# Halo V summed chunk by chunk, half of the FFN weights cast DRAM to DRAM ahead of use, and V scratch on the sync queue, in a hybrid decoder layer on eight cores

## The chip, the cores and the metric

The kernel runs as one program on the eight NeuronCores of one Trainium2 chip (two dies of four cores). The metric is the device time of the slowest core, in microseconds. A run is called slow when one die runs over 1% longer at a lower granted TensorE clock, or when the run is over 1.5% above the fastest of its kernel; ratios and intervals use fast runs alone.

## The reference, cut to what matters

One decoder layer on x of shape (4, 8192, 1024). Each core takes half a sequence: 8 "own" tiles of 512 tokens, preceded by 4 "halo" tiles, of which only K and V are needed.

```python
h = rmsnorm(x, g_mix)
q, k, v, u, qm = split(h @ w_in, ...)            # 512, 512, 512, 256, 256 columns
y_attn = dilated_window_attention(q, k, v)       # (128,1), (512,4), (2048,16), merged
y_pool = causal_multiscale_pool(u) @ w_pool * pool_scale
y_mem  = softmax(qm @ km.T) @ vm                 # km, vm from 256 memory tokens
x = x + concat(y_attn, y_pool, y_mem) @ w_out
x = x + relu(rmsnorm(x, g_ffn) @ w_ff1)**2 @ w_ff2   # 1024 -> 4096 -> 1024
return rmsnorm(x, g_final)
```

## The kernel before

Weights come in pieces of 128 x 4096 values. A piece is 2 MiB in f32 in DRAM (`wall`) and 1 MiB in bf16. A ring of three slots in SBUF holds the pieces. The first use of a piece is a casting load from `wall` on the POOL queue; it is then written back as bf16 to a DRAM scratch (`sc`), and later uses are bf16 loads on the sync (SP) queue. Half of the FFN pieces are not written back at their first use ("deferred"), so they are loaded from f32 twice, in the first and the second own tile.

```python
deferred = {P_FF1 + i for i in range(1, 8, 2)} | {P_FF2 + i for i in range(1, 8, 2)}
def ring_issue():
    ...
    if idx in done:
        T.dma("sp", ring_sem[s], ring[s][:], sc[idx], reads=[b_scp[idx]], writes=[b_ring[s]])
    else:
        T.dma("pool", cast_sem[s], ring[s][:], wall[idx], writes=[b_ring[s]])
        if idx in deferred:
            deferred.discard(idx)
            return
        done.add(idx)
        T.dma("sp", wb_sem[s], sc[idx], ring[s][:], reads=[b_ring[s]], writes=[b_scp[idx]])
```

V is needed in two token orders. From the last halo tile on, each of four V blocks is evicted from PSUM, written to a DRAM scratch `vs` (192 KB each) and read back in the other order into `Vd4` (768 KB). Attention of a tile cannot use its own Vd4 before this read has landed.

```python
T.dma("pool", vsw_sem[b], vs[j % 2][b * 128:(b + 1) * 128, :], dst, reads=bd, ...)   # four times
...
def read_v():
    for t_ in toks:                      # the four writes
        T.wait("pool", t_)
    T.dma("pool", vsr_sem[j % 2], Vd4[:, slot, :, :].rearrange("p r e -> p (r e)"),
          vs[j % 2].rearrange("(c r) e -> c (r e)", r=4), ...)
```

`T.wait` and `T.dma` run in program order on the queue's own engine: a wait holds up everything that this engine issues later (in the change, below, the sync queue on core 1 issued nothing from 125.2 to 173.95 us while it waited for writes of V). Every tile starts with a LayerNorm-like statistic (`LN`: squares on ACT, adds on DVE, one matmul with ones, then norms on DVE). A halo tile then runs four V groups of eight matmuls and four K groups.

The softmax here doesn't subtract the row's maximum and nothing guards it: scores larger than these inputs give would overflow.

## Time and profile before

1661.23 us, median of 3 runs (1658.43 to 1662.81). TensorE is busy for 93% of the span, and from 480 us on for about 98% of each 200 us, so the loss sits in the first 480 us.

The rows of the page for TensorE and the DMA engines, in 40 equal slices of 41.5 us; a digit is the busy share in tenths:

```profile
PE   3889899989799999999999999999999999998996
...
PEclk9999999999999999999999999999999999998998
DMA  9828578995857675354835375344734373434342
```

The first slice is a third busy, and slices 9 and 11 (332 to 374 and 415 to 457 us) dip. The reasons are in the waits of TensorE on the slowest core, core 1 (what it waited for: us in total, times, longest):

```profile
PE mm L336 <- DVE acc L362: 38.9, 8, 19.5
...
PE mm L336 <- DMA ring<-wall: 9.9, 3, 4.7
PE mm L336 <- DMA ring<-wscratch: 9.4, 2, 7.3
```

It waits 38.9 us for the LayerNorm sum (19.5 of it at the start), and 19.3 us for weights in the ring. The timeline of TensorE shows where (start, duration, instruction, count; in brackets the idle time before it and what ended it):

```profile
341.44 1.89 PE L336 MATMUL mm<-aT,ring 128*128 128x512 bf16 x8 [1.94 <-DMA ring<-wall]
...
370.11 9.90 PE L336 MATMUL mm<-aT,ring 128*128 128x512 bf16 x32 [4.65 <-DMA ring<-wall]
...
435.82 3.61 PE L336 MATMUL mm<-h2T,ring 128*128 128x512 bf16 x16 [3.34 <-DMA ring<-wall]
...
451.65 4.95 PE L336 MATMUL mm<-h2T,ring 128*128 128x512 bf16 x16 [7.35 <-DMA ring<-wscratch]
```

These four gaps are 17.3 us. The matmuls after the 4.65 us gap took 9.90 us for 32, where 32 take 7.07 us elsewhere. The granted clock, from the trace by stretch, was 0.71 over these 9.90 us: 0.50 from 370.1 to 375.6, where in the kept trace the matmuls start 0.427 us apart, and 0.97 from there to 380.0, where they start 0.216 us apart. So about 5.5 us went at half rate. After the 7.35 us gap the clock was 0.50 for 2.5 us, and 16 matmuls took 4.95 us; after the 3.34 us gap it was 1.00, and 16 took 3.61 us.

### The profile page before, as it was taken

The numbers are of one execution on the slowest core, as the hardware profiler recorded it, in microseconds if no ns is written. First come the engines' busy times: TensorE is split into PE (matmuls) and PEld (weight loads), VectorE is DVE, ScalarE is ACT, GpSimd is POOL, SyncE is SP. The second block draws the span as 40 slices with busy tenths as digits, with TensorE's granted clock in tenths as the row PEclk, the third lists the DMA queues.
The fourth block names the chain that finished last, engine by engine and source line by source line (L and its number), as shares of the span: only waits on it lengthen the run. The fifth ranks groups of instructions, "written<-read, shape, count | busy, mean of one in ns | idle before, by whom it ended". The sixth has DMA issues, their size and how long they took to land.

```text
span 1660.2 us, 27812 instructions; the slowest of 8 cores (1640.5 to 1660.2 us)
## 1 busy us (share of the span) xinstructions
PE 1548.5 (93%) x9722; PEld 748.0 (45%) x9722; DVE 930.2 (56%) x1383; ACT 715.5 (43%) x1069; POOL 137.2 (8%) x189
## 2 busy tenths in 40 slices
PE   3889899989799999999999999999999999998996
PEld 1434544444355444454454444454445444453442
DVE  5666566546365466656465556656565555546333
ACT  3545654532444336443444436343444335442221
POOL 1102110101000010000100010000100000000000
PEclk9999999999999999999999999999999999998998
DMA  9828578995857675354835375344734373434342
GB/s 227 227 87 263 131 153 165 198 203 174 245 152 201 180 219 200 105 176 138 276 107 178 110 233 178 128 153 166 253 114 167 128 234 122 163 130 152 139 152 90
DMA packets 41081, 282.93 MB, mean 170 GB/s; under 512 B 5248, under 2 KB 5376, under 8 KB 8560
## 3 DMA queue, kind: packets, MB, share of 16 engines
q1 hardware_dynamic: 24048, 172.01, 30.6%
q0 software_dynamic: 16896, 109.13, 25.6%
q8 instruction: 81, 1.33, 0.3%
q14 instruction: 56, 0.46, 0.1%
HBM read 266.77 MB, written 46.92 MB: 189 GB/s over the span
## 4 chain that ended last, share of the span: by engine, by line
PE 80%; DMA 7%; DVE 5%; issue 4%; ACT 4%; ACTq 0%; DVEq 0%; POOL 0%; SPq 0%; POOLq 0%
PE mm L336 70%; PE ob L577 6%; PE sc L554 4%; DMA ring<-wall 3%; DMA ring<-wscratch 2%; ACT P L556 2%; DVE acc L362 1%; ACT sq L360 1%; DMA wscratch<-ring 1%; DVE val L588 1%; DMA out<-X 1%; DVE X L709 1%; DVE X L374 0%; DMA cpc_t<-cpc 0%; ACT rt L686 0%
## 5 line engine op out<-in xcount | busy, mean ns | idle before, releaser
L336 PE MATMUL mm<-h2T,ring 128*128 128x512 bf16 x2192 | 511.0, 383 | 13.9 <-DMA ring<-wscratch 7.3
L336 PE MATMUL mm<-aT,ring 128*128 128x512 bf16 x2048 | 474.2, 382 | 24.5 <-DVE X L709 15.9
L689 DVE TENSOR_TENSOR aT<-rt 128x512 bf16<-128x512 f32 x256 | 199.9, 783 | 242.6 <-ACT rt L686 241.1
L556 ACT ACTIVATE P<-sc 128x1024 bf16<-128x1024 f32 x256 | 247.7, 1023 | 184.4 <-PE sc L554 178.7
L336 PEld LDWEIGHTS mm<-h2T,ring 128*128 128x128 bf16 x2192 | 206.7, 98 | 256.3 <-issue 32.7
L336 PEld LDWEIGHTS mm<-aT,ring 128*128 128x128 bf16 x2048 | 192.6, 98 | 249.5 <-issue 42.8
L686 ACT ACTIVATE rt<-mm 128x512 f32<-128x512 f32 x256 | 153.0, 598 | 272.2 <-PE mm L336 250.7
L561 DVE TENSOR_TENSOR P<-P,E 128x1024 bf16<-128x1024 bf16 x224 | 154.0, 694 | 127.6 <-ACT P L556 126.5
L360 ACT ACTIVATE sq<-X 128x512 f32<-128x512 f32 x196 | 122.4, 630 | 161.3 <-DVE X L709 102.5
L362 DVE TENSOR_TENSOR acc<-acc,sq 128x512 f32<-128x512 f32 (+1 forms) x203 | 142.9, 705 | 73.6 <-ACT sq L360 71.1
L336 PE MATMUL mm<-hT,ring 128*128 128x512 bf16 x704 | 156.3, 383 | 0.5 <-DVE KT L343 0.5
L709 DVE TENSOR_TENSOR X<-X,mm 128x512 f32<-128x512 f32 x128 | 87.6, 685 | 119.2 <-PE mm L336 118.6
L577 PE MATMUL ob<-P,Vd 128*128 128x128 bf16 x1792 | 136.7, 219 | 9.6 <-DVE val L588 7.8
L577 PEld LDWEIGHTS ob<-P,Vd 128*128 128x128 bf16 x1792 | 116.1, 98 | 64.9 <-issue 20.9
L592 POOL TENSOR_TENSOR yT<-val,den 128x512 bf16<-128x512 f32 x48 | 62.4, 1300 | 772.6 <-DVE val L588 240.0
L336 PE MATMUL mm<-yT,ring 128*128 128x512 bf16 x512 | 114.8, 383 | 2.7 <-POOL yT L592 2.1
L336 PEld LDWEIGHTS mm<-hT,ring 128*128 128x128 bf16 x704 | 69.2, 99 | 87.2 <-issue 8.2
L336 PEld LDWEIGHTS mm<-yT,ring 128*128 128x128 bf16 x512 | 49.8, 98 | 68.4 <-issue 12.3
L374 DVE SCALAR_TENSOR_TENSOR h2T<-X,gc,acc 128x512 bf16<-128x512 f32 x88 | 61.7, 745 | 27.8 <-ACT acc L370 23.5
L554 PE MATMUL sc<-Q,KT 64*128 64x128 bf16 x1792 | 71.8, 219 | 2.0 <-ACT P L556 1.3
L588 DVE COPY val<-ob 64x512 f32<-64x512 f32 x96 | 65.9, 687 | 13.1 <-PE ob L577 11.1
L336 PE MATMUL mm<-ring,hT 128*128 128x512 bf16 x288 | 68.6, 389 | 3.1 <-DVE hT L374 2.5
(70 smaller groups left out, 785.1 us busy)
## 6 DMA issues: line engine op xcount, KB each, us to landing
ring<-wscratch SPq DMA_DIRECT2D x142, 1024.0 KB, 5.9
ring<-wall POOLq DMA_DIRECT2D x29, 1024.0 KB, 12.0
X<-xh POOLq DMA_DIRECT2D x24, 1024.0 KB, 10.5
wscratch<-ring SPq DMA_DIRECT2D x21, 1024.0 KB, 7.3
X<-xr POOLq DMA_DIRECT2D x16, 1024.0 KB, 7.1
out<-X POOLq DMA_DIRECT2D x16, 1024.0 KB, 9.9
Vd<-vscratch POOLq DMA_DIRECT2D x10, 768.0 KB, 7.8
vscratch<-Vd POOLq DMA_DIRECT2D x32, 192.0 KB, 7.1
```

The costliest lines, as they stand in the source:

```text
L336: T.op("pe", lambda: nc.tensor.matmul(out_ap, lhsT=l, rhs=r, start=(i == 0), stop=(i == n - 1)), reads=rd, writes=[b_out], mark=(i == n - 1))
L360: T.op("act", lambda: nc.scalar.activation(out=s_, in_=self.x3[:, k, :], func=AF.Square), reads=[self.b_x[k]], writes=[bs_])
L362: T.op("dve", lambda: nc.vector.tensor_tensor(out=self.acc, in0=self.acc, in1=s_, op=ALU.add), reads=[bs_], writes=[self.b_acc])
L554: T.op("pe", lambda: nc.tensor.matmul(o2, lhsT=l[lo:lo + 64], rhs=rr, start=True, stop=True), reads=bt["qk_reads"], writes=[bs_], mark=(i ...
L556: T.op("act", lambda: nc.scalar.activation(out=P_[:], in_=s_[:], func=AF.Exp, scale=0.125), reads=[bs_], writes=[bP_])
L561: T.op("dve", lambda: nc.vector.tensor_tensor(out=Pv, in0=Pv, in1=m, op=ALU.mult), reads=[bP_, b_E, b_E16], writes=[bP_])
L577: T.op("pe", lambda: nc.tensor.matmul(o_, lhsT=l[:, v0:v0 + 128], rhs=r_, start=(bt["first"] and i == 0), stop=(bt["last"] and i == n - 1) ...
L588: T.op("dve", lambda: nc.vector.tensor_copy(out=val[lo:lo + 64, :], in_=ob[hh][lo:lo + 64, :]), reads=[b_ob[hh]], writes=[b_val[hh]])
L592: T.op("pool", lambda: nc.gpsimd.tensor_tensor(out=yT[:, ch, :], in0=val[:], in1=den[:], op=ALU.mult), reads=b_den + b_val, writes=[b_yT[ch]])
L686: T.op("act", lambda: nc.scalar.activation(out=rt[i][:, 0:TOK], in_=m_[:], func=AF.Relu), reads=[bm_], writes=[b_rt[i]])
L689: T.op("dve", lambda: nc.vector.tensor_tensor(out=aT[:, a_, :], in0=rt[i][:, 0:TOK], in1=rt[i][:, 0:TOK], op=ALU.mult), reads=[b_rt[i]], w ...
L709: T.op("dve", lambda: nc.vector.tensor_tensor(out=xi[:, d, :], in0=xi[:, d, :], in1=m_[:], op=ALU.add), reads=[bm_], writes=[bxi[d]])
```

## The change

Its intent is threefold. (a) Shorten the start: x comes in quarters, four square buffers let ACT run ahead of DVE, the constant columns of V go to POOL, the V groups of a halo tile run side by side in four PSUM banks so that they start with the first chunk of h, and the memory-token group moves from the last halo tile to the first own tile. (b) Cast eight FFN pieces DRAM to DRAM before they are needed, so that no piece is loaded twice from f32. (c) Take V scratch out of the POOL queue, where it waited among other things, and put it on sync.

```diff
-        load_x("pool", 1, xh[0])
+        for h in range(4):
+            T.dma("pool", x0_sem[h], X[1][:, 2 * h:2 * h + 2, :], xh[0][:, 2 * h:2 * h + 2, :], ...)
...
-        deferred = {P_FF1 + i for i in range(1, 8, 2)} | {P_FF2 + i for i in range(1, 8, 2)}
+        ahead = [P_FF1 + 1, P_FF1 + 3, P_FF2 + 1, P_FF2 + 3, P_FF1 + 5, P_FF1 + 7, P_FF2 + 5, P_FF2 + 7]
+        def cast_ahead(n):
+            for _ in range(n):
+                idx = ahead.pop(0)
+                T.dma("pool", ahead_sem.pop(), sc[idx], wall[idx], writes=[b_scp[idx]])
+                done.add(idx)
...
+            def vsweep(q):                       # chunks 2q, 2q+1 of h into four banks
+                ...
+            groups += [vsweep(q) for q in range(4)] if j < NHALO else [vgroup(b, b == 3) for b in range(4)]
...
-                        T.dma("pool", vsw_sem[b], vs[j % 2][b * 128:(b + 1) * 128, :], dst,
+                    T.dma("sp", vsw_sem[b], vs[j % 2][b * 128:(b + 1) * 128, :], dst,
...
-                    T.wait("pool", t_)
-                T.dma("pool", vsr_sem[j % 2], Vd4[...], vs[j % 2]...)
+                    T.wait("sp", t_)
+                T.dma("sp", vsr_sem[j % 2], Vd4[...], vs[j % 2]...)
...
+        side += [(0, lambda: cast_ahead(2)), (7.9, lambda: cast_ahead(2))]     # first own tile
+        run(stage_B(j) + mg, side)                                             # mg: memory group, moved here
         load_x("pool", j % 2, xr[0])
         load_x("pool", (j + 1) % 2, xh[j + 2])
...
+            cast_ahead(4)                        # just before attention of the first own tile
             att_over(j, b2[0:12])
```

More of the change, by code (lines that the diff above doesn't have):

```diff
@@ L172, in build_nc @@
         x_sem = {q: [[dsem(f"xsem_{q}{i}_{h}") for h in range(2)] for i in range(2)] for q in ("sp", "pool")}
+        x0_sem = [dsem(f"x0sem{h}") for h in range(4)]
         out_sem = [[dsem(f"osem{i}_{h}") for h in range(2)] for i in range(2)]
@@ L189, in build_nc @@
         b_acc = bufs("acc", 2)
+        ACC = [(acc[i], [b_acc[i]]) for i in range(2)]
+        SQ = [(sq[i], b_sq[i]) for i in range(2)]
+        SQ_EARLY = SQ + [(Pbuf[i][:].rearrange("p h t -> p (h t)").bitcast(F32), b_P[i]) for i in range(2)]
         kmT = sb("kmT", [128, 2, 256], BF16)
@@ L207, in build_nc @@
         b_ob = bufs("ob", 2)
+        SC_EARLY = [(scb[i // 2][:, i % 2, :], b_sc[i // 2]) for i in range(4)]
         b_scp = bufs("scp", NPIECES)
@@ L248, in load_w @@
             T.dma("pool", cast_sem[SLOT[pi]], ring[SLOT[pi]][:], wall[pi], writes=[b_ring[SLOT[pi]]])
-        load_x("pool", 1, xh[0])
+        for h in range(4):
+            T.dma("pool", x0_sem[h], X[1][:, 2 * h:2 * h + 2, :], xh[0][:, 2 * h:2 * h + 2, :], writes=b_X[1][2 * h:2 * h + 2])
         load_w(P_V)
@@ L255, in build_nc @@
             for r in range(4):
-                T.op("dve", lambda: nc.vector.tensor_copy(
+                T.op("pool", lambda: nc.gpsimd.tensor_copy(
                     out=Vd4[:, s_, r, :].rearrange("p (c s d) -> p c s d", c=4, s=3)[:, :, 1, :],
@@ L260, in build_nc @@
             g = (4 * (NHALO - 1) + b) % 5
-            T.op("dve", lambda: nc.vector.tensor_copy(
+            T.op("pool", lambda: nc.gpsimd.tensor_copy(
                 out=Vd1[:, g, :].rearrange("p (c s d) -> p c s d", c=4, s=3)[:, :, 1, :],
@@ L288, in build_nc @@
         done = {P_V, P_K, P_UM, P_Q}
-        deferred = {P_FF1 + i for i in range(1, 8, 2)} | {P_FF2 + i for i in range(1, 8, 2)}
+        ahead = [P_FF1 + 1, P_FF1 + 3, P_FF2 + 1, P_FF2 + 3, P_FF1 + 5, P_FF1 + 7, P_FF2 + 5, P_FF2 + 7]
+        ahead_sem = [dsem(f"aheadsem{i}") for i in range(len(ahead))]
+        def cast_ahead(n):
[3 more added lines that the diff above has]
+                done.add(idx)
         for j in range(NHALO, NT):
@@ L307, in ring_issue @@
                 T.dma("pool", cast_sem[s], ring[s][:], wall[idx], writes=[b_ring[s]])
-                if idx in deferred:
-                    deferred.discard(idx)
-                    return
                 done.add(idx)
@@ L346, in build_nc, with __init__ @@
         class LN:
-            def __init__(self, x3, b_x, gi, out3, b_out, n=TOK):
+            def __init__(self, x3, b_x, gi, out3, b_out, acc_, n=TOK, early=False):
                 self.x3, self.b_x, self.gi, self.out3, self.b_out, self.n = x3, b_x, gi, out3, b_out, n
-                i = 1 if gi in (G_FIN, G_MEM) else 0
-                self.acc, self.b_acc = acc[i][:, 0:n], b_acc[i]
+                self.acc, self.b_acc = acc_[0][:, 0:n], acc_[1]
+                self.sq = SQ_EARLY if early else SQ
+                self.first = None
@@ L352, in square @@
             def square(self, k):
-                if k == 0:
-                    T.op("act", lambda: nc.scalar.activation(out=self.acc, in_=self.x3[:, 0, :], func=AF.Square),
-                         reads=[self.b_x[0]], writes=[self.b_acc])
-                    return
-                i = cnt["sq"] % 2
+                i = cnt["sq"] % len(self.sq)
                 cnt["sq"] += 1
-                s_, bs_ = sq[i][:, 0:self.n], b_sq[i]
+                s_, bs_ = self.sq[i][0][:, 0:self.n], self.sq[i][1]
@@ L360, in square @@
                 T.op("act", lambda: nc.scalar.activation(out=s_, in_=self.x3[:, k, :], func=AF.Square),
                      reads=[self.b_x[k]], writes=[bs_])
+                if k == 0:
+                    self.first = (s_, bs_)
+                    return
+                if k == 1:
+                    a_, ba_ = self.first
+                    T.op("dve", lambda: nc.vector.tensor_tensor(out=self.acc, in0=a_, in1=s_, op=ALU.add),
+                         reads=[ba_, bs_], writes=self.b_acc)
+                    return
@@ L362, in square @@
                 T.op("dve", lambda: nc.vector.tensor_tensor(out=self.acc, in0=self.acc, in1=s_, op=ALU.add),
-                     reads=[bs_], writes=[self.b_acc])
+                     reads=[bs_], writes=self.b_acc)
             def stat(self):
                 m_, bm_ = next_mm()
-                mm_ops(m_[:, 0:self.n], bm_, [(ones[:], self.acc, [b_ones, self.b_acc])])
+                mm_ops(m_[:, 0:self.n], bm_, [(ones[:], self.acc, [b_ones] + self.b_acc)])
                 T.op("act", lambda: nc.scalar.activation(out=self.acc, in_=m_[:, 0:self.n], func=AF.Ln, bias=EPS),
-                     reads=[bm_], writes=[self.b_acc])
+                     reads=[bm_], writes=self.b_acc)
@@ L370, in stat @@
                 T.op("act", lambda: nc.scalar.activation(out=self.acc, in_=self.acc, func=AF.Exp, scale=-0.5),
-                     reads=[self.b_acc], writes=[self.b_acc])
+                     reads=self.b_acc, writes=self.b_acc)
             def norm(self, k):
@@ L376, in norm @@
                     op0=ALU.mult, op1=ALU.mult),
-                    reads=[self.b_x[k], self.b_acc, b_g], writes=[self.b_out[k]])
+                    reads=[self.b_x[k], b_g] + self.b_acc, writes=[self.b_out[k]])
         def hbuf(j):
@@ L386, in stage_A @@
             i = (j + 1) % 2
-            return LN(X[i], b_X[i], G_MIX, h3, bh)
+            if j > NHALO + 1:
+                return LN(X[i], b_X[i], G_MIX, h3, bh, ACC[0])
+            return LN(X[i], b_X[i], G_MIX, h3, bh, ACC[j % 2], early=True)
         def stage_B(j):
@@ L405, in take, with sweep, h_tok, f @@
                     st[name] = (piece[:].rearrange("p (k c) -> p k c", k=8), [b_])
+            def sweep(trips, outs, q):
+                for k in (2 * q, 2 * q + 1):
+                    for trip, (o_, bo_) in zip(trips, outs):
+                        mm_ops(o_, bo_, trip, k, k + 1)
+            def h_tok(b, k):
+                if j < NHALO - 1:
+                    return h3[:, k, :].rearrange("p (a s) -> p a s", s=4)[:, :, b]
+                return h3[:, k, b * 128:(b + 1) * 128]
+            def vsweep(q):
+                def f():
+                    if q == 0:
+                        take("v", P_V)
+                    pk, bp = st["v"]
+                    sweep([[(h_tok(b, k), pk[:, k, :], bp + [bh[k]]) for k in range(8)] for b in range(4)], SC_EARLY, q)
+                    if q == 3:
+                        for b in range(4):
+                            vevac(b, b == 3, *SC_EARLY[b])
+                return f
+            def usweep(q):
+                def f():
+                    if q == 0:
+                        take("u", P_UM)
+                    pk, bp = st["u"]
+                    sweep([[(pk[:, k, ol * 128:(ol + 1) * 128], h3[:, k, :], bp + [bh[k]]) for k in range(8)]
+                           for ol in range(4)], SC_EARLY, q)
+                    if q == 3:
+                        for ol in range(4):
+                            fevac(P_UM, ol, *SC_EARLY[ol])
+                return f
             def vgroup(b, last):
@@ L412, in f @@
                     m_, bm_ = next_mm()
-                    if j < NHALO - 1:
-                        def hs(k):
-                            return h3[:, k, :].rearrange("p (a s) -> p a s", s=4)[:, :, b]
-                    else:
-                        def hs(k):
-                            return h3[:, k, b * 128:(b + 1) * 128]
-                    mm_ops(m_[:], bm_, [(hs(k), pk[:, k, :], bp + [bh[k]]) for k in range(8)])
-                    if j < NHALO - 1:
-                        dst, bd = Vd4[:, slot, b, :], [b_Vd4[slot]]
-                    elif j == NHALO + 1:
-                        dst, bd = vt[:, b, :], [b_vt[b]]
-                        bd[0].r = bd[0].r + [t_ for a_ in b_aT[8:16] for t_ in a_.r]
-                    else:
-                        g = (4 * j + b) % 5
-                        dst, bd = Vd1[:, g, :], [b_Vd1[g]]
@@ L428, in f @@
-                    d4 = dst.rearrange("p (c s d) -> p c s d", c=4, s=3)
-                    evac("dve" if j == NHALO + 1 else "act", d4[:, :, 0::2, :],
-                         m_[:].rearrange("p (c s d) -> p c s d", c=4, s=2), [bm_], bd)
-                    if NHALO <= j <= NHALO + 1:
-                        T.op("dve", lambda: nc.vector.memset(d4[:, :, 1, :], 1.0), writes=bd)
-                    if j >= NHALO - 1:
-                        T.dma("pool", vsw_sem[b], vs[j % 2][b * 128:(b + 1) * 128, :], dst,
-                              reads=bd, writes=[b_vs[j % 2]] if b == 0 else [])
-                        toks.append((vsw_sem[b].sem, vsw_sem[b].val, "dma"))
@@ L437, in f, with vevac @@
-                    if last:
-                        if j > NHALO:
-                            ring_issue()
-                        if j >= NHALO - 1 and j != NHALO + 1:
-                            read_v()
-                return f
+                    mm_ops(m_[:], bm_, [(h_tok(b, k), pk[:, k, :], bp + [bh[k]]) for k in range(8)])
+                    vevac(b, last, m_[:], bm_)
+                return f
+            def vevac(b, last, m_, bm_):
+                if j < NHALO - 1:
+                    dst, bd = Vd4[:, slot, b, :], [b_Vd4[slot]]
+                elif j == NHALO + 1:
+                    dst, bd = vt[:, b, :], [b_vt[b]]
+                    bd[0].r = bd[0].r + [t_ for a_ in b_aT[8:16] for t_ in a_.r]
+                else:
+                    g = (4 * j + b) % 5
+                    dst, bd = Vd1[:, g, :], [b_Vd1[g]]
+                d4 = dst.rearrange("p (c s d) -> p c s d", c=4, s=3)
+                evac("dve" if j == NHALO + 1 else "act", d4[:, :, 0::2, :],
+                     m_.rearrange("p (c s d) -> p c s d", c=4, s=2), [bm_], bd)
+                if NHALO <= j <= NHALO + 1:
+                    T.op("dve", lambda: nc.vector.memset(d4[:, :, 1, :], 1.0), writes=bd)
+                if j >= NHALO - 1:
+                    T.dma("sp", vsw_sem[b], vs[j % 2][b * 128:(b + 1) * 128, :], dst,
+                          reads=bd, writes=[b_vs[j % 2]] if b == 0 else [])
+                    toks.append((vsw_sem[b].sem, vsw_sem[b].val, "dma"))
+                if last:
+                    if j > NHALO:
+                        ring_issue()
+                    if j >= NHALO - 1 and j != NHALO + 1:
+                        read_v()
@@ L444, in read_v @@
             def read_v():
                 for t_ in toks:
-                    T.wait("pool", t_)
-                T.dma("pool", vsr_sem[j % 2], Vd4[:, slot, :, :].rearrange("p r e -> p (r e)"),
+                    T.wait("sp", t_)
+                T.dma("sp", vsr_sem[j % 2], Vd4[:, slot, :, :].rearrange("p r e -> p (r e)"),
                       vs[j % 2].rearrange("(c r) e -> c (r e)", r=4), reads=[b_vs[j % 2]], writes=[b_Vd4[slot]])
@@ L451, in read_v @@
                         a_.r = a_.r + toks
-                    T.dma("pool", vsr1_sem, Vd1[:, 0:4, :], vs[j % 2].rearrange("(b p) e -> p b e", p=128),
+                    T.dma("sp", vsr1_sem, Vd1[:, 0:4, :], vs[j % 2].rearrange("(b p) e -> p b e", p=128),
                           reads=[b_vs[j % 2]], writes=b_Vd1[0:4])
@@ L464, in f @@
                     mm_ops(m_[:], bm_, [(pk[:, k, ol * 128:(ol + 1) * 128], h3[:, k, :], bp + [bh[k]]) for k in range(8)])
-                    if pi == P_K:
-                        evac("dve" if own else "act", KT[:, ol, slot * TOK:(slot + 1) * TOK], m_[:], [bm_], [b_KT[slot]])
-                    elif pi == P_Q:
-                        evac("act", Q[:, ol, :].rearrange("p (r c) -> p r c", r=4),
-                             m_[:].rearrange("p (c r) -> p r c", r=4), [bm_], [b_Q[ol]])
-                    elif ol < 2:
-                        evac("dve", U[:, ol, 16:16 + TOK], m_[:], [bm_], [b_U])
-                    else:
-                        evac("dve" if j == NHALO + 1 else "act", QM[:, ol - 2, :].rearrange("p (r c) -> p r c", r=4),
-                             m_[:].rearrange("p (c r) -> p r c", r=4), [bm_], [b_QM[ol - 2]])
+                    fevac(pi, ol, m_[:], bm_)
                     if last and own and not (j == NHALO or (j == NHALO + 1 and pi == P_Q)):
@@ L477, in fgroup, with fevac @@
                 return f
-            groups += [vgroup(b, b == 3) for b in range(4)]
+            def fevac(pi, ol, m_, bm_):
+                if pi == P_K:
+                    evac("dve" if own else "act", KT[:, ol, slot * TOK:(slot + 1) * TOK], m_, [bm_], [b_KT[slot]])
+                elif pi == P_Q:
+                    evac("act", Q[:, ol, :].rearrange("p (r c) -> p r c", r=4),
+                         m_.rearrange("p (c r) -> p r c", r=4), [bm_], [b_Q[ol]])
+                elif ol < 2:
+                    evac("dve", U[:, ol, 16:16 + TOK], m_, [bm_], [b_U])
+                else:
+                    evac("dve" if j == NHALO + 1 else "act", QM[:, ol - 2, :].rearrange("p (r c) -> p r c", r=4),
+                         m_.rearrange("p (c r) -> p r c", r=4), [bm_], [b_QM[ol - 2]])
+            groups += [vsweep(q) for q in range(4)] if j < NHALO else [vgroup(b, b == 3) for b in range(4)]
             if j == NHALO + 1:
@@ L485, in stage_B @@
             if j == NHALO:
-                groups = [fgroup("u", P_UM, ol, False) for ol in range(4)] + groups
+                groups = [usweep(q) for q in range(4)] + groups
             groups += [fgroup("k", P_K, ol, ol == 3) for ol in range(4)]
@@ L780, in mem_groups, with __getitem__ @@
             pk = aT_hi.rearrange("p (k c) -> p k c", k=8)
-            mT = Q[:].rearrange("p a t -> p (a t)").rearrange("p (k t) -> p k t", k=8)
-            b_mT = bufs("mT", 8)
-            for b in b_mT:
-                b.w = None
-            ln = LN(memf, b_yT, G_MEM, mT, b_mT, n=256)
+            mT = [Pbuf[2 + k // 4][:].rearrange("p h t -> p (h t)")[:, (k % 4) * 256:(k % 4) * 256 + 256] for k in range(8)]
+            b_mT = [b_P[2 + k // 4] for k in range(8)]
+            class MemOut:
+                def __getitem__(self, at):
+                    return mT[at[1]]
+            ln = LN(memf, b_yT, G_MEM, MemOut(), b_mT, (val, b_val), n=256, early=True)
             def kgroup(mp):
                 m_, bm_ = next_mm()
-                mm_ops(m_[:, 0:256], bm_, [(pk[:, k, mp * 128:(mp + 1) * 128], mT[:, k, :], b_aT[8:16] + [b_mT[k]])
+                mm_ops(m_[:, 0:256], bm_, [(pk[:, k, mp * 128:(mp + 1) * 128], mT[k], b_aT[8:16] + [b_mT[k]])
                                            for k in range(8)])
@@ L794, in vgroup @@
                 m_, bm_ = next_mm()
-                mm_ops(m_[:, 0:256], bm_, [(mT[:, k, kc * 128:(kc + 1) * 128], pk[:, k, 256:512], b_aT[8:16] + [b_mT[k]])
+                mm_ops(m_[:, 0:256], bm_, [(mT[k][:, kc * 128:(kc + 1) * 128], pk[:, k, 256:512], b_aT[8:16] + [b_mT[k]])
                                            for k in range(8)])
@@ L798, in vgroup @@
                      m_[:, 0:256].rearrange("p (c s d) -> p c s d", c=2, s=2), [bm_], [b_vm])
-                for b in b_Q:
-                    b.r = [t for t in b.r] + [b_mT[0].r[-1]]
             return ln, [lambda: kgroup(0), lambda: kgroup(1), lambda: vgroup(0), lambda: vgroup(1)]
@@ L808, in build_nc @@
         for j in range(NHALO):
-            if j + 2 < NHALO:
+            if j < 2:
                 load_x("pool", (j + 3) % 2, xh[j + 2])
-            if j == 0:
+            if j == 1:
                 load_w(P_UM)
-            if j == 1:
-                mem_loads()
-                load_q()
             if j == 2:
                 load_x("pool", 1, xh[NHALO])
-                const_loads()
-            if j == 3 and n_own > 1:
-                load_x("pool", 0, xh[NHALO + 1])
-            nxt = stage_A(j + 1)
-            side = ln_side(nxt, 0, 0.5, 4, 4.5, 0.5)
-            groups = stage_B(j)
-            if j == 3:
-                mln, mg = mem_groups()
-                side += ln_side(mln, 2.2, 0.5, 6.2, 6.7, 0.4)
-                groups += mg
-            run(groups, side)
+                mem_loads()
+            if j == 3:
+                if n_own > 1:
+                    load_x("pool", 0, xh[NHALO + 1])
+                load_q()
+                const_loads()
+            side = ln_side(stage_A(j + 1), 0, 0.5, 5, 5.5, 0.3) if j else ln_side(stage_A(1), 4, 0.25, 6, 6.5, 0.2)
+            run(stage_B(j), side)
             if j == NHALO - 1:
@@ L835, in build_nc @@
         two = n_own > 1
+        mln, mg = mem_groups()
         side = [(8, lambda: [T.wait("sp", (T.sem["pe"], T.cnt["pe"], "pe"))]
                  + [write_back(p_) for p_ in (P_V, P_K, P_UM, P_Q)])]
+        side += ln_side(mln, 0, 0.5, 5, 5.5, 0.4)
         if two:
-            side += ln_side(stage_A(j + 1), 0, 0.5, 5, 5.5, 1)
-        side += [(3 + 0.8 * i, f) for i, f in enumerate(pool_steps(j))]
-        run(stage_B(j), side)
+            side += ln_side(stage_A(j + 1), 8, 0.5, 13, 14.5, 0.5)
+        side += [(4 + 0.7 * i, f) for i, f in enumerate(pool_steps(j))]
+        side += [(0, lambda: cast_ahead(2)), (7.9, lambda: cast_ahead(2))]
+        run(stage_B(j) + mg, side)
         load_x("pool", j % 2, xr[0])
@@ L851, in build_nc @@
                 ring_issue()
+            cast_ahead(4)
             att_over(j, [])
@@ L857, in build_nc @@
             last = j + 1 == NT
-            ln2 = LN(X[j % 2], b_X[j % 2], G_FFN, h2T, b_h2T)
+            ln2 = LN(X[j % 2], b_X[j % 2], G_FFN, h2T, b_h2T, ACC[0])
             first = j == NHALO
@@ L872, in build_nc @@
             run(groups, side)
-            fin = LN(X[j % 2], b_X[j % 2], G_FIN, X[j % 2], b_X[j % 2])
+            fin = LN(X[j % 2], b_X[j % 2], G_FIN, X[j % 2], b_X[j % 2], ACC[1])
             side = [(50 + 2 * d + 0.5, lambda d=d: fin.square(d)) for d in range(8)]
```

## The prediction

> **What bounds the kernel now.** From 480 us on, TensorE is busy about 98% of each 200 us window (busy time by stretch), so little is to be had there. The loss is in the first 480 us. The timeline of the slowest core shows TensorE without work for 19.5 us at the start, then 2.4 to 4.1 us in each halo stage before the LayerNorm statistic (waits: 32 us behind the DVE accumulator), and 17.3 us of waits for ring weights at 341, 366, 432 and 444 us. Other cores lose 9 to 18 us to ring weights. After a long gap matmuls run at half rate for some microseconds: 32 took 9.9 us after the 4.7 us gap against 7.07 us[...].
>
> **What the change does.**
>
> 1. First tile. x in quarters, four square buffers, ones-columns on POOL: DVE no longer spends 5.2 us ahead of its adds. The last half of x lands at 12.6 us, so the statistic moves from 19.5 to about 15 us, and V sums start at about 19.4 instead of 24.05. But the V weights land only at 19.0 and the K weights at 31.8 us (issue plus landing); DMA is full from 4 to 40 us. The V sweep ends near 28.5, then TensorE waits for K. The next tile's squares now come after four V evictions and between K evictions on ACT, so the second statistic stays near 40 to 42 us, though two K groups (3.5 us) precede it. Stage 1 starts at about 47.5 as before: gain 0 to 3 us.
> 2. Halo stages 1 and 2. The statistic moves behind one K group (1.7 us), but one square waits behind four V evictions (2.2 us). The gap shrinks only from 2.4 to about 1.8 us: gain 1 us in all.
> 3. Stages 3 and 4 (83.8 to 148.0 us, 53 us of pure matmul work). The memory group leaves stage 3, where it cost some 4 us of waits, for stage 4, where DVE gets crowded. I expect 21 + 37 us instead of 31.6 + 32.6: gain 6 us.
> 4. Ring. Eight FFN pieces are cast once, DRAM to DRAM, while DMA is nearly idle (100 to 140 us), instead of twice from f32; the second own tile reads only bf16. Most of the 17.3 us plus 4 us of half-rate matmuls should go: gain 17 us.
> 5. New cost. The last four casts (an estimate from the 6.3 us that a 2 MiB f32 piece takes at full DMA rate, plus its 1 MiB write: 6 to 9 us each) stand in the queue ahead of the first output-projection piece; it may come 0 to 10 us late at about 190 us: loss 4 us.
>
> Sum: 1 + 1 + 6 + 17 + 1 (POOL free of V waits) - 4 = about 22, and some 5 more because the slowest core lost the most to the ring. Predicted 1634 us, 1616 to 1650. Chances: faster by over 2% 0.35, within 2% 0.61, slower 0.04.
>
> **What would show it.** Right: no ring waits over 2 us between 330 and 460 us; attention of the first own tile starting near 141 us instead of 148; K groups of stage 0 waiting for DMA until about 31 us. Wrong: ring waits at the first output projection over 10 us, or stage 1 starting well before 45 us.
>
> **What would make it wrong.** DRAM-to-DRAM casts much slower than loads; the sync queue, which now waits for V writes, delaying weight loads in the steady stage; DVE overload in stage 4 costing over 4 us.

The half rate is the one measured above; the "4 us of half-rate matmuls" are what the matmuls after the 4.65 and 7.35 us gaps took beyond 7.07 and 3.61 us (2.83 and 1.34 us). For the 6.3 us of point 5 the trace of the kernel before shows 6.2 us on core 1: the V weights landed at 18.98 and the K weights at 31.78, 6.17 and 6.23 us after the transfer ahead of each in the queue, and the DMA engines' busy share from 4 to 40 us is 1.01.

## More of the kernel before

DMA issues of V scratch in the kernel before (KB each, median us from issue to landing), from the page's list of DMA issues:

```profile
ring<-wall POOLq DMA_DIRECT2D x29, 1024.0 KB, 12.0
...
Vd<-vscratch POOLq DMA_DIRECT2D x10, 768.0 KB, 7.8
vscratch<-Vd POOLq DMA_DIRECT2D x32, 192.0 KB, 7.1
```

## The result

1710.89 us, median of 4 runs (1708.49 to 1714.55), against 1661.94 for the kernel before (the three runs above and one more): the ratio of the fast runs is 1.0301, with a 95% interval of 1.0273 to 1.0328. It is 3% slower, outside the predicted range. (Ratios here are the mean time of one kernel's fast runs over that of the other's of the same rounds, so not quite the ratio of the medians.) The profiled run is fast, and its slowest core is core 1 again, so the two traces compare core for core.

The same rows of the page as before; a slice is now 42.7 us:

```profile
PE   3886089999999999999999999999999999998996
...
PEclk9999599999999999999999999999999999999998
DMA  7799986685843447343833456343834363344342
```

The fifth slice (171 to 213 us) has a zero: TensorE does nothing while the DMA engines are over 90% busy. The granted clock there is 0.5, with TensorE busy for 2.7 of 42 us (171 to 213 us, from the trace by stretch). It is 0.50 from 163.5 to 214.7 us and 1.00 from there to 220, and the following slices are back at 0.9 or more. The waits of TensorE name it:

```profile
PE ob L631 <- DMA Vd<-vscratch: 50.5, 1, 50.5
PE mm L349 <- DVE acc L380: 38.2, 8, 18.1
PE mm L349 <- DMA ring<-wscratch: 17.4, 7, 3.9
...
PE mm L349 <- DMA ring<-wall: 1.2, 1, 1.2
```

A single wait of 50.5 us for Vd is new. The waits for f32 pieces (ring<-wall) are nearly gone, as intended, and the waits for bf16 pieces went from 9.4 us in 2 waits to 17.4 us in 7. The timeline shows the long one in the middle of the attention of the first own tile:

```profile
159.04 0.77 PE L608 MATMUL sc<-Q,KT 64*128 64x128 bf16 x16
210.30 1.86 PE L631 MATMUL ob<-P,Vd 128*128 128x128 bf16 x16 [50.49 <-DMA Vd<-vscratch]
...
251.94 1.67 PE L349 MATMUL mm<-yT,ring 128*128 128x512 bf16 x7
```

What was V scratch doing? The timeline of the sync queue's issues in the change:

```profile
92.70 2.49 SPq L100 DMA_DIRECT2D vscratch<-Vd  x4
122.62 0.32 SPq L100 DMA_DIRECT2D Vd<-vscratch  x1
123.04 2.15 SPq L100 DMA_DIRECT2D vscratch<-Vd  x4
173.95 0.32 SPq L100 DMA_DIRECT2D Vd<-vscratch  x1
```

V of the first own tile is written at 123.0 to 125.2 us, but its read can be issued only at 173.95, when the four writes have landed, 49 us later. The writes did not move all that time: in the same queue, 0.4 us ahead of them, stood the V read of the last halo tile (issued at 122.62). By the packet records of the kept trace, the packets of that read started from 128.8 to 152.8, and those of the writes only from 151.8 to 168.8. So V was held up twice beside the casts, first the halo's read and then the own tile's. The chain of work that ended last, from 120 to 215 us, has the same two steps (start, us, what):

```profile
124.73 49.15 DMA vscratch<-Vd
173.95 35.95 DMA Vd<-vscratch
210.30 1.86 PE ob L631 x16
```

The casts are the other traffic at that time. Here are the POOL queue's issues of casts in the change, from the timeline:

```profile
90.41 2.04 POOL L100 DMA_DIRECT2D wscratch<-wall  x4
...
149.11 1.99 POOL L100 DMA_DIRECT2D wscratch<-wall  x4
```

And the landing of the last cast of the second four, from the list of DMA issues (count, KB, us from issue to landing):

```profile
wscratch<-wall POOLq DMA_DIRECT2D x1, 1024.0 KB, 59.2
```

Issued at about 150.6, this last cast landed 59.2 us later, at 209.8. The V read landed at 209.9 (173.95 + 35.95). The casts take about 10 us each: the first of each four landed after 32.3 and 29.7 us, the fourth after 61.2 and 59.2 us.

The steady tiles got longer too. From the first output-projection matmul of one own tile to the next, it is 185.1 us before in the fifth own tile (951.04 to 1136.15) and 187.5 us after in the fifth and sixth (996.12 to 1371.13 for the two). The balance on core 1 adds up: the first output projection starts 50.5 us later (201.46, now 251.94), the first own tile from there to the second takes 4.4 us less (178.4, now 174.0), the second 9.7 us less (200.7, now 191.0), and the rest of the program 11.0 us more (1079.6, now 1090.6): +47.4, against 47.3 us between the two spans.

### The profile page after: what moved, and what is told of

Same layout as the page of the kernel before. It is cut to its first block, busy times and chain, and to the rows that moved or that the text cites. A ratio compares the mean times of both kernels' runs of the same rounds, so it can differ in the third digit from the quotient of the medians.

```text
span 1707.5 us, 27804 instructions; the slowest of 8 cores (1684.2 to 1707.5 us)
## 1 busy us (share of the span) xinstructions
PE 1544.1 (90%) x9722; PEld 748.5 (44%) x9722; DVE 928.8 (54%) x1367; ACT 712.8 (42%) x1069; POOL 116.9 (7%) x153
## 3 DMA queue, kind: packets, MB, share of 16 engines
q0 software_dynamic: 11472, 85.79, 21.4%
## 4 chain that ended last, share of the span: by engine, by line
PE 73%; DMA 15%; ACT 4%; DVE 4%; issue 3%; POOL 0%; SPq 0%; ACTq 0%; DVEq 0%; POOLq 0%
PE mm L349 62%; PE ob L631 6%; DMA ring<-wscratch 6%; DMA vscratch<-Vd 5%; PE sc L608 3%; DMA ring<-wall 2%; DMA Vd<-vscratch 2%; ACT P L610 2%; PE sc L349 2%; DVE val L642 1%; ACT Vd L354 1%; DVE X L763 1%; DVE X L392 0%; ACT rt L740 0%; DVE acc L380 0%
## 5 line engine op out<-in xcount | busy, mean ns | idle before, releaser
L349 PE MATMUL mm<-h2T,ring 128*128 128x512 bf16 x2192 | 514.0, 384 | 19.7 <-DMA ring<-wscratch 16.7
L349 PE MATMUL mm<-aT,ring 128*128 128x512 bf16 x2048 | 469.5, 379 | 16.0 <-DVE X L763 15.9
L740 ACT ACTIVATE rt<-mm 128x512 f32<-128x512 f32 x256 | 152.8, 597 | 280.8 <-PE mm L349 258.8
L631 PE MATMUL ob<-P,Vd 128*128 128x128 bf16 x1792 | 137.4, 220 | 60.0 <-DMA Vd<-vscratch 50.5
L349 PE MATMUL mm<-hT,ring 128*128 128x512 bf16 x672 | 149.2, 382 | 6.1 <-DVE KT L356 2.7
L380 DVE TENSOR_TENSOR acc<-acc,sq 128x512 f32<-128x512 f32 x144 | 104.3, 724 | 42.8 <-ACT sq L370 41.3
L349 PEld LDWEIGHTS mm<-hT,ring 128*128 128x128 bf16 x672 | 65.6, 98 | 89.4 <-issue 14.3
L608 PEld LDWEIGHTS sc<-Q,KT 64*128 64x128 bf16 x1792 | 53.7, 107 | 39.9 <-issue 36.9
```

The lines of the kernel that those rows point to most:

```text
L349: T.op("pe", lambda: nc.tensor.matmul(out_ap, lhsT=l, rhs=r, start=(i == 0), stop=(i == n - 1)), reads=rd, writes=[b_out], mark=(i == n - 1))
L380: T.op("dve", lambda: nc.vector.tensor_tensor(out=self.acc, in0=self.acc, in1=s_, op=ALU.add), reads=[bs_], writes=self.b_acc)
L608: T.op("pe", lambda: nc.tensor.matmul(o2, lhsT=l[lo:lo + 64], rhs=rr, start=True, stop=True), reads=bt["qk_reads"], writes=[bs_], mark=(i ...
L631: T.op("pe", lambda: nc.tensor.matmul(o_, lhsT=l[:, v0:v0 + 128], rhs=r_, start=(bt["first"] and i == 0), stop=(bt["last"] and i == n - 1) ...
L740: T.op("act", lambda: nc.scalar.activation(out=rt[i][:, 0:TOK], in_=m_[:], func=AF.Relu), reads=[bm_], writes=[b_rt[i]])
```

## Experiments

Theory A: V scratch is starved by the casts because each DMA engine serves the two queues in turns, and a turn of the cast queue is long. This was my guess: no trace shows the turns themselves, and casts cut into other sizes are to test it. Theory B: the bytes of the casts fill the engines or the memory, so that any V transfer is late at that time. Theory C: the sync queue itself, waiting in order for something else, held V up. All twelve runs gave correct results.

### The two halves of the suspicion, apart and together

Put V scratch back on POOL (`v_pool`), take the casts out and restore the deferred pieces (`no_cast`), or both (`v_pool_no_cast`, which leaves only part (a) of the change).

```diff
 v_pool:   -T.dma("sp", vsw_sem[b], ...)   +T.dma("pool", vsw_sem[b], ...)     # and the waits and the reads
 no_cast:  -ahead = [...]                  +deferred = {the same eight}; cast_ahead does nothing
 v_pool_no_cast: both
```

> The change with V scratch back on the POOL queue, casts kept. Theory A (the V transfers starve on the sync queue because they take turns, packet by packet, with the big cast packets of the other queue): V now stands in one queue with the casts and simply waits for the first four (about 149 us), then goes before the second four. The 50.5 us wait for Vd of the first own tile falls to under 8 us. The second four casts then stand before the first output-projection piece, so a ring wait of 5 to 17 us may appear near 200 us. Steady ring waits (17.4 us behind ring<-wscratch) go too. About 1650 to 1660 us. Theory B (the casts flood the memory, whoever issues V): the wait for Vd stays at 30 to 50 us, about 1690 us.

> The change without the casts ahead (the odd FFN pieces are loaded twice from f32 as before), V scratch on sync. Both theories A and B: the 50.5 us wait is gone, V writes and read land in under 8 us each. The ring waits of before (17 us near 340 to 450 us) come back, at least in part. If the sync queue is what costs 17.4 us of small ring waits in the steady tiles, they stay. About 1665 to 1675 us. Theory C (the sync queue itself, blocked in order behind other waits, holds V up): the wait of 50 us stays without casts.

> Only the halo part of the change: no casts ahead, V scratch on POOL. Attention of the first own tile starts at 146 to 147 us instead of 148, everything after is as before. 1655 to 1662 us against 1661.

| kernel | casts | V queue | median us | ratio to before, 95% interval |
|---|---|---|---|---|
| the change | yes | sync | 1710.89 | 1.0301 (1.0273 to 1.0328) |
| v_pool | yes | POOL | 1668.37 | 1.0058 (1.0040 to 1.0076) |
| no_cast | no | sync | 1666.07 | 1.0044 (1.0017 to 1.0072) |
| v_pool_no_cast | no | POOL | 1656.62 | 0.9994 (0.9971 to 1.0016) |

The 50 us wait needs both: without casts, the V read of the first own tile issued at 122.58 on the sync queue landed in 5.8 us (core 6; 5.3 to 7.0 on the eight cores), so theory C is out. Part (a) alone is worth nothing that these runs can tell from zero. In v_pool the wait for Vd is gone, but the waits of TensorE (core 3, the slowest) show another one:

```profile
PE mm L349 <- DMA ring<-wall: 36.4, 2, 33.7
```

The 33.7 us wait ends at 232.85, at the first output-projection matmul. The piece it waits for was issued behind the casts in the same queue, and the DMA issue of that moment shows it:

```profile
ring<-wall POOLq DMA_DIRECT2D x1, 1024.0 KB, 71.2
```

It landed 71.2 us after its issue. In v_pool the V writes waited behind the first two casts (POOL waited 23.3 us for them), so six casts of 10 us each and the x loads stood ahead of this piece. So casts and V on POOL exchange a 50 us wait for one of 27.1 to 34.3 us on the eight cores. My expectation had the mechanism but only 5 to 17 us of it. This run alone does not prove the turns, as it also moves the casts: POOL waits for the halo's V first and issues its first cast at 109.94 instead of 90.41.

### Does a turn of the cast queue hold V up?

`cast_rows` described each cast as 1024 rows of 2 KiB.

```diff
-T.dma("pool", ahead_sem.pop(), sc[idx], wall[idx], ...)
+T.dma("pool", ahead_sem.pop(), sc[idx].rearrange("p (a c) -> (p a) c", a=8), wall[idx].rearrange(...), ...)
```

> The change exactly, but each DRAM to DRAM cast is described as 1024 rows of 2 KiB f32 instead of 128 rows of 16 KiB: same bytes, queue and order of issue. Theory A: a V packet waits for a packet of an eighth the size, so V writes and read of the first own tile land in under 15 us each instead of 49 and 36, and the 50.5 us wait falls below 15 us. Theory B (bytes, not packets): wait stays at 40 to 50 us. If the rows are joined again by the hardware (packet count unchanged), the run says nothing.

1704.54 us (ratio 1.0280), with 11,472 packets on the POOL queue as in the change: the rows were joined again, and the run says nothing, as foreseen. `cast_split8` and `cast_split4` instead cut each cast into 8 or 4 DMAs, at the same place in the queue:

```diff
+for r_ in range(0, 128, 16):     # cast_split4: steps of 32 rows
+    T.dma("pool", a_, sc[idx][r_:r_ + 16, :], wall[idx][r_:r_ + 16, :])
```

> The change exactly (V scratch on sync, same casts at the same places), but each cast is issued as 8 DMAs of 16 rows, one row for each of the 16 DMA engines. Bytes and order unchanged. Theory A (the queues of one DMA engine take turns, and a turn of the cast queue is as long as a share of one cast DMA): the turn shrinks, the V read of the first own tile lands in under 15 us instead of 36, the 50.5 us wait falls below 20 us, total under 1680 us. Theory B (the bytes of the casts fill the DMA engines, no matter how they are cut): wait 40 to 55 us, total 1700 to 1712 us.

> The change with each cast issued as 4 DMAs of 32 rows (2 rows for each DMA engine). If a turn of the cast queue is one DMA's share on an engine, V's read of the first own tile (10.4 us with 8 DMAs a cast, 36 with one) lands in 15 to 25 us. If it lands in 30 us or more, or in 11 or less, that rule is wrong.

The V read of the first own tile in the list of DMA issues (count, KB, us from issue to landing), in the change on core 1:

```profile
Vd<-vscratch SPq DMA_DIRECT2D x1, 768.0 KB, 36.0
```

The same read in the list of cast_split4, on core 2:

```profile
Vd<-vscratch SPq DMA_DIRECT2D x1, 768.0 KB, 19.7
```

In that of cast_split8, on core 5:

```profile
Vd<-vscratch SPq DMA_DIRECT2D x1, 768.0 KB, 10.4
```

And in that of no_cast, on core 6:

```profile
Vd<-vscratch SPq DMA_DIRECT2D x1, 768.0 KB, 5.8
```

Before these are compared, one has to look up what ran beside each read. The kept traces hold every DMA packet with its size and duration (no view of `prof` lists them). In the change a cast is recorded as 32 packets of 32 KB of bf16 (four rows), 4.7 us each in the median during this read; in cast_split4 as packets of 16 KB, 2.2 us; in cast_split8 as packets of 8 KB (one row), about 1.05 us. In cast_rows they are still of 32 KB. Between issue and landing of the read, 96 cast packets started in the change (core 1), and 97, each half as large, in cast_split4 (core 2): six for each of the 16 DMA engines on average in both. The read took 36.0 and 19.7 us (18.6 to 20.5 on the eight cores of cast_split4), and in cast_split4 the casts went on until 217 us. The wait for Vd fell with it, from 50.5 to 19.6 us (17.7 to 20.9 on the eight cores). Theory B had said that cutting the casts changes nothing (40 to 55 us of wait): it is out.

The 10.4 us of cast_split8 (10.4 to 12.6 on the eight cores) do not belong in this row. There the read ran beside the x loads, not the casts: the first of the second four casts landed at 169.5 to 179.4 us, after the read (159.4 to 166.1) on every core, and the first four had landed before its first packet started. That it met the expectation was luck. The same holds for cores 6 and 7 of the change, where 14 cast packets and none started during the read, which landed in 12.3 and 13.0 us. A read of cast_split8 that did run beside casts is the one before, of the last halo tile. The same four kernels in the order of above (cores 1, 2, 5 and 6):

```profile
Vd<-vscratch SPq DMA_DIRECT2D x1, 768.0 KB, 31.2
...
Vd<-vscratch SPq DMA_DIRECT2D x1, 768.0 KB, 22.4
...
Vd<-vscratch SPq DMA_DIRECT2D x1, 768.0 KB, 15.9
...
Vd<-vscratch SPq DMA_DIRECT2D x1, 768.0 KB, 4.0
```

On the eight cores it is 21.7 to 31.8, 20.5 to 22.4, 14.6 to 15.9 and 4.0 to 5.3 us: the finer the cut, the sooner V lands. So the sizes fit a turn of one cast packet, though the turns themselves were not shown. In the change such a packet is half of a cast DMA's share on an engine (8 rows), not the whole of it. Nor did V only land when the casts were over, though the two times are close on core 1 (209.9 and 209.8 us): the 128 packets of the read started all through the casts, from 180.8 to 209.1, and seven of eight had started by 204.8.

The total of cast_split8 was 1688.71 us (fast runs 1683.90 to 1689.73; ratio 1.0178, interval 1.0157 to 1.0200), above the expected 1680, because behind the wait for Vd stood the other one, on the slowest core (core 5):

```profile
PE mm L352 <- DMA ring<-wall: 19.6, 2, 17.2
...
PE ob L634 <- DVE val L645: 16.3, 21, 8.6
```

The first output-projection piece was 17.2 us late (14.4 to 21.2 us on the eight cores), and TensorE lost another 8.6 us to a DVE copy in this attention. That copy reuses a buffer which POOL has to read first. The kept trace shows POOL issuing 32 cast DMAs from 151.34 to 166.81, reading the buffer (L649) right after, and the copy starting when that was done. What the copy waited for, from 150 to 172 us:

```profile
DVE val L645 <- POOL yT L649: 9.7, 1, 9.7
```

So cutting the casts has a price of its own, the time to issue them. cast_split4, one run, took 1687.51 us.

### What V on sync costs the steady tiles

Each steady tile of the change waits for bf16 pieces. In the third own tile, on core 1, the sync queue issued the V read at 649.27 and the first FFN piece at 649.74, and TensorE then waited 2.85 us for that piece at 665.12. `no_cast_read_late` issues the read after that piece:

```diff
 in the last K group of a steady tile:
                         ring_issue()
+                        if pi == P_K and j > NHALO + 1:
+                            read_v()          # and no longer after the last V group
```

> The run without casts (V scratch on sync), with V's read in the steady tiles issued after the weight load that follows the K groups, instead of before it. Theory: there the sync queue sends V's read (768 KB, 10.8 us) in front of the first feed-forward piece, which is then 3 us late in each tile. Expected: ring<-wscratch waits fall from 16.9 us (8 waits) to under 6 us, total 5 to 10 us shorter than the run without casts (1666), about 1656 to 1661. Rival (the sync engine's in-order waits for V's writes, or the writes themselves, delay the loads): the waits stay.

1651.27 us, ratio 0.9969 (0.9945 to 0.9993), against 1666.07 of no_cast; each ratio is to the kernel before of its own chip. The waits of TensorE for bf16 pieces from 480 us on in no_cast (core 6):

```profile
PE mm L347 <- DMA ring<-wscratch: 8.9, 6, 2.2
```

And the same waits in no_cast_read_late (core 0):

```profile
PE mm L347 <- DMA ring<-wscratch: 1.5, 1, 1.5
```

The steady waits went from 8.9 to 1.5 us by moving one read behind one load, so the read's place in the queue was the cause, and the writes and the sync engine's waits, which stayed, were not. On the eight cores the waits were 0 to 13.6 us and are 0 to 1.6; cores 0 and 1 of no_cast had none with the read in front, and why is open. The total gained more than the 5 to 10 us expected. Much of the surplus lies in the second own tile, which took 195.9 us in no_cast and 186.2 in no_cast_read_late (slowest cores): in no_cast seven cores waited 5.9 to 8.9 us for a piece of the ring at 420 to 431 us, in no_cast_read_late no core waited over 2.2 us between 400 and 480, though it loads the same pieces from f32 and casts none ahead. So the ring waits of that tile, which the casts were to remove, also went when V's read stood elsewhere.

### Versions that keep what is good

`early4` has V on POOL and casts only four pieces (FF1+1, FF1+3, FF2+1, FF2+3), after V's read of the first own tile; the other four are deferred as before. `early4_late4` casts the other four one by one behind the f32 pieces of the first own tile. `early4_second` casts the other four early instead and defers the first. `early4_mix` is early4 with V on sync, read late, from the third own tile on.

```diff
-side += [(0, lambda: cast_ahead(2)), (7.9, lambda: cast_ahead(2))]
+side += [(7.9, lambda: cast_ahead(4))]       # V on POOL; the later cast_ahead(4) is gone
```

> Halo part kept, V scratch on POOL, only four of the eight casts, all issued after V's read of the first own tile and ahead of the x loads; the other four pieces are loaded twice from f32 as before. At 10 us a cast they end near 164 us, x near 177, and the first output-projection piece lands near 185, before it is needed at 200. Expected: no ring wait at 200 us, no wait for Vd; ring waits at 340 to 450 us 5 to 10 us instead of 17. 1643 to 1653 us.

> As the run before, with the other four casts issued one by one behind the first four f32 feed-forward pieces of the first own tile. If DMA has room for a 10 us cast in every 17 us there, all ring waits of 340 to 450 us go: 1638 to 1648 us. If not, waits of 3 to 8 us show between 250 and 340 us and it is no better than the run before.

> As early4, but the four pieces cast ahead are those of the second half of the feed-forward part, whose f32 loads were the late ones (waits at 341 and 370 us). Expected: those two waits (7 us, and some 3 us of half-rate matmuls behind them) go, no wait for Vd and none over 3 us at 200 us; 1636 to 1646 us, against 1649 of early4. Rival (the lateness only moves with the number of f32 loads, not with which): waits of about 7 us somewhere between 205 and 460 us, 1647 to 1651 us.

> early4 with V scratch on POOL only while casts are in flight (the halo and the first two own tiles) and on sync, read after the next weight load, from the third own tile on. If what V on POOL costs in the steady tiles is the difference between the no-cast runs with V on sync and late read (1651) and V on POOL (1657), this is 3 to 6 us faster than early4. If that difference came from the first 480 us or from chance, it is within 2 us of early4.

> early4 once more, in more rounds and beside the run above: ratio 0.993 to 0.997 to before.

| kernel | median us | ratio to before, 95% interval |
|---|---|---|
| early4 | 1648.98 | 0.9947 (0.9925 to 0.9969) |
| early4_again | 1649.58 | 0.9954 (0.9939 to 0.9969) |
| early4_second | 1652.71 | 0.9965 (0.9947 to 0.9983) |
| early4_mix | 1652.12 | 0.9971 (0.9954 to 0.9987) |
| early4_late4 | 1775.56 (fast runs near 1666) | 1.0055 (1.0031 to 1.0078) |

early4 is 0.5% faster than the kernel before in two sets of rounds, and so far faster than the change. Part of this needs no cast at all: no_cast_read_late, on the same chip and in the same rounds, has 1651.27 against 1648.98 us, and their intervals overlap. Its remaining ring waits on the slowest core, from the timeline:

```profile
341.69 1.89 PE L353 MATMUL mm<-aT,ring 128*128 128x512 bf16 x8 [1.88 <-DMA ring<-wall]
...
370.91 9.88 PE L353 MATMUL mm<-aT,ring 128*128 128x512 bf16 x31 [5.20 <-DMA ring<-wall]
```

early4_second removes these two and gets others, at the second own tile, whose first-half pieces now come from f32 again (core 2, its slowest):

```profile
430.69 3.61 PE L353 MATMUL mm<-h2T,ring 128*128 128x512 bf16 x16 [2.80 <-DMA ring<-wall]
...
446.45 5.25 PE L353 MATMUL mm<-h2T,ring 128*128 128x512 bf16 x16 [7.27 <-DMA ring<-wscratch]
```

So which pieces are cast moves the wait between the two tiles, as the rival of its expectation had said. early4_late4 shows that there is no room for casts among the FFN loads of the first own tile: a wait of 17.2 us for a bf16 piece came at 278.94. Two of its four runs were slow, which lifts the median; the ratio uses the fast ones. early4_mix was no faster than early4, so V on sync, read late, is not worth having in the steady tiles. The 5 us between the medians of the two no-cast kernels (read late on sync, 1651.27; V on POOL, 1656.62) may be chance: they ran on different chips and their intervals overlap.

## Why the prediction was wrong, point by point

- **The step that failed** is the one that costed V scratch on the sync queue at nothing: the sum books "1 (POOL free of V waits)" for it as a gain, and the list of doubts has only "the sync queue, which now waits for V writes, delaying weight loads in the steady stage". I asked who waits in program order, and did not ask what the casts would do to a read on the other queue: it landed in 36.0 us beside cast packets of 32 KB, in 19.7 us beside packets of 16 KB and in 5.8 us without casts. The term was +1 us; measured, it is one wait of 50.5 us beside the casts, and 2.3 to 5.7 us in each of the third to sixth own tiles on core 1 (for example 187.5 against 185.1). The doubt about weight loads was right, but it is the small part.
- **Point 5, the casts ahead of the output projection, was mis-sized.** Predicted 0 to 10 us late with 6 to 9 us a cast. A cast took about 10 us. In the change the V wait hid the lateness, as TensorE came to the output projection only at 251.94. Taken out of its shade it was 27 to 34 us (v_pool) or 14 to 21 us (cast_split8).
- **Point 4, the ring, held in mechanism.** Waits for f32 pieces fell from 9.9 to 1.2 us (though a wait of 3.9 us for a bf16 piece, at 385, broke the limit of 2 us that I had set), and the first two own tiles, from output projection to output projection and beyond, took 14.1 us less (4.4 + 9.7) where 17 was expected, although V on sync cost the second tile something. v_pool needs 8.4 us less than v_pool_no_cast for the first own tile (170.9 and 179.3 us) and 11.1 us less for the second (185.1 and 196.2), each on its slowest core.
- **Points 1 and 2 had the order of events, but gained less.** The timeline of TensorE after, through the halo stages:

```profile
18.10 2.05 PE L349 MATMUL mm<-acc,ones 128*128 128x512 f32 x2 [18.10 <-DVE acc L380]
22.62 9.19 PE L349 MATMUL sc<-ring,hT 128*128 128x512 bf16 x32 [2.48 <-DVE hT L392]
33.04 3.61 PE L349 MATMUL mm<-hT,ring 128*128 128x512 bf16 x16 [1.23 <-DMA ring<-wall]
42.38 2.05 PE L349 MATMUL mm<-acc,ones 128*128 128x512 f32 x2 [5.73 <-DVE acc L380]
...
49.27 7.07 PE L349 MATMUL sc<-ring,h2T 128*128 128x512 bf16 x32
...
60.30 1.27 PE L349 MATMUL mm<-acc,ones 128*128 128x512 f32 x2 [2.23 <-DVE acc L380]
```

  The V sums start at 22.62 (24.05 before, 19.4 expected: the first x quarter was late here, and ACT began its squares at 11.21 only). The K groups then wait for their weights until 33.04, and the second statistic comes at 42.38. Stage 1 starts at 49.27, against 47.54 before and 47.5 expected, so 1.7 us were lost where 0 to 3 were to be gained: the earlier start was swallowed by 1.23 us of wait for the K weights and by 5.73 us for the second statistic (2.62 before). The halo gap shrank from 2.38 to 2.23 us; 1.8 was expected.
- **Point 3 was too hopeful.** Stage 3 took 20.1 us (85.24 to 105.29; 21 expected), but stage 4 with the memory group took 41.5 us (to 146.75; 37 expected), 3.2 us of it in waits of TensorE for DVE's evictions of K and 2.1 us in waits for the two statistics. Attention started at 146.75 instead of 147.96, not at 141.
- **Sums of mean values miss such a failure.** The range, 1616 to 1650 us, was made of small, independent terms. What came was one large term, on a path that the change itself had put at risk.

Left open: whether the engines do serve the queues in turns, and if so how many V packets pass in one turn, as between the first and the last of the 8 on each engine only about 5 cast packets started in the change (80 over 16 engines, core 1) and about 4 in cast_split4 (65, core 2); and why cores 0 and 1 of no_cast had no steady waits.

## What to carry to other kernels

Before moving a small, urgent transfer to another queue, look at what the DMA engines will be doing when it is issued: here large DMAs in one queue made a 768 KB transfer in the other take up to 36 us, and cutting them so that a packet had two rows instead of four brought it to about 20. When such transfers are compared, check first what ran beside each: the best-looking read of cast_split8 had met no cast. Casts that "fill idle DMA time" are only free if nothing that someone waits for is issued, in any queue, before they end (here TensorE waited 50.5 us for V on sync, and 33.7 us for weights behind the casts with V on POOL); write down for each queue what stands ahead of the next needed piece. And when a long wait is taken away, expect the next one behind it: here the late output-projection weights stood behind the late V.

What these runs measured, for use elsewhere:

- Cast packets of 8, 16 and 32 KB (bf16) took about 1.05, 2.2 and 4.7 us, and a 768 KB read on sync landed in 4.0 to 7.0 us without casts, in 14.6 to 15.9, 18.6 to 22.4 and up to 36.2 us beside DRAM-to-DRAM casts of 1 MiB (bf16) on the POOL queue cut into 8, 4 and 1 DMAs.
- The choice of the queue decided what a transfer waits behind: TensorE waited 50.5 us for Vd with V on sync and not at all with V on POOL, with the same casts (slowest cores).
- A casting DRAM-to-DRAM DMA, with all eight cores at it, took about 10 us for 2 MiB of f32 to 1 MiB of bf16, beside about 6.2 us for a casting load of such a piece into SBUF (kernel before, core 1: it landed at 18.98 us, the transfer ahead of it in the queue at 12.81).
